# Taking GpSimd's reads of SBUF out of the pooling stage of a two-layer encoder step

## The chip, the cores and the metric

One launch on one core of a Trainium2 chip. The metric is the device time of that launch in microseconds (us), as the median of several runs. The five engines of the core are TensorE (PE in the profile; PEld is its weight load), VectorE (DVE), ScalarE (ACT), GpSimd (POOL) and SyncE (SP, which here only issues DMAs).

## The reference, cut to what matters

Two equal layers work on 576 columns: 512 frames of a new stream ("prompt") and 64 further frames of a running stream ("sample", with 1024 cached frames). All numbers are float32.

```
h = rms_norm(x, norm_g);  proj = h @ w_in            # 1024 inputs, 5416 columns of weights
u_p, z_p, q, k, v, qi, ki, wi, z_a, g_p, g_a = split(proj)
pooled   = for 4 groups of 128 channels: mean over the last 2, 4, 8, 16 frames of u_p, minus u_p
br_pool  = ((pooled @ w_pool_mix) * pool_scale * silu(z_p)) @ w_pool_out
score    = sum_heads wi * relu(rope(qi) @ rope(ki).T * 32**-0.5) * 8**-0.5
sel      = the best 128 (prompt) or 256 (sample) keys of each row of score
o        = softmax over sel of rope(q) @ rope(k).T * 64**-0.5, times v
x        = x + (sigmoid(g_p) * br_pool + sigmoid(g_a) * ((o * silu(z_a)) @ w_attn_out)) @ w_o
```

The new keys, values, indexer keys and the last 15 rows of u_p are outputs too. After layer 2 a last rms_norm gives y.

## The kernel before, in words

Channels lie on the 128 partitions and the 576 columns along the free dimension, as two halves of 288. Weights come in pieces of 128 x 1024 float32 (512 KB), 58 in each layer. TensorE takes float32 operands rounded to its own format, so each operand is split into a rounded high part and a low part (value minus high part), and each product is made of three matmuls: high by high, high by low, low by high. One piece is 48 matmuls of 288 columns. The high part of a piece is made by a ScalarE copy; the low part by a second, negated ScalarE copy, onto which a DMA of the POOL queue adds the raw piece (`split_to`). The first piece alone is done by halves with subtractions on VectorE and GpSimd (`split_first`). Raw pieces have a ring of three buffers (`raws`), split pieces a ring of three (`whl`).

Everything is issued through a planner (`Plan`, lines 66 to 250). It keeps an estimated free time for each engine from a cost formula for each operation, and it emits waiting jobs (`pump`) between the matmuls of a product where it believes that their inputs are ready. So the estimates set the order of the instructions on every engine, and an engine then runs its list strictly in that order. The formulas hold no term for one engine slowing another. `psum_free`, `need` and `room` are its conditions; four PSUM banks ("sm") serve small products and two double banks ("mm") the weight products.

The stages of a layer, in the order of the pieces:

- **Entry.** x is rounded (`h`), its low part made, and squared (`sq`); the squares are summed in `acc` for the norm. In layer 1 this runs while x arrives (`first`); `FIRST_H` names the k for which VectorE rounds instead of ScalarE, and `FIRST_POOL` those whose square GpSimd adds. The same eight steps multiply the key weights `kiw` and the first query piece. `norm_a` reduces `acc` by matmuls with ones and takes the root, `norm_b` spreads the result over all partitions as `Rt`.
- **Pooling stage.** Pieces u0 to u3 and z0 to z3 (`u_job`, `z_job`). VectorE scales the product (`ux`), builds window sums and `pl`; ScalarE rounds `pl` into `ph`; the low part follows. z is turned into a gate `sg` (sigmoid on ScalarE, then a product). Six matmuls per group mix (`sm<-quart 128x288` in the trace), and the result `av` is split into `ah` and `al`. Between these stand the index scores: 24 products for the prompt (`sm<-quart,big`, 256, 384 and 512 columns wide), each passed by ScalarE as relu into a `prob` buffer and added up by VectorE (`SCALAR_TENSOR_TENSOR quart<-prob,wcol,quart`).
- **Selection.** VectorE alone: 16 rounds of MAX8 and MATCH_REPLACE8 for the prompt, then 12 sample score products of 364 or 360 columns, then 32 rounds for the sample. The result of the sample's selection is needed only by the sample attention at the end.
- **Gates, attention, outputs.** gp, po, then k, q, v pieces with the prompt's attention between them, then za, ga with the sample's attention, then the two output products. GpSimd has the rotary products of k and other products there.

In the pooling stage of before, GpSimd does the small copies into `ux` and `pst`, the low parts of `ph`, of the mixing weights `wmx` and of `al`, and the gate product. At the end of layer 1, `prepare_ki` loads the next layer's raw key weights into one of the three `raw` buffers.

All operations go through one recording helper, so every instruction has line L263; the tile names tell them apart.

Of the kernel before, what the change touches and what calls it, by code (L numbers as in the profile page):

```python
# [10 lines left out]
F32 = mybir.dt.float32  # L11
F32R = mybir.dt.float32r
AF = mybir.ActivationFunctionType
OP = mybir.AluOpType
# [3 lines left out]
TP = 512  # L18
TS = 64
T = TP + TS  # L20
# [26 lines left out]
UNITS = 3  # L47
FIRST_H = (1, 3, 5, 7)
FIRST_POOL = (1, 2, 3)
LAG = (1, 2)  # L50
# [218 lines left out]
def encoder_step(ctx: ExitStack, tc: tile.TileContext, a: dict):  # L269
# [86 lines left out]

    def split_first():

        x = raw_of.pop(0)
        w = rot.tile([P, 2, 1024], F32R, name="whl", tag="whl", bufs=3)  # L360
        for c, eng in ((slice(0, 512), dve), (slice(512, 1024), pool)):
            act.copy(w[:, 0, c], x[:, c])
            eng.tensor_tensor(w[:, 1, c], x[:, c], w[:, 0, c].bitcast(F32), op=OP.subtract)
        plan.let(x)
        split_of[0] = w
        state["split"] = 1

# [178 lines left out]
    def prepare_ki(l):  # L546
        rk = raws()
        rki = rk[:, :320].rearrange("p (k c) -> p k c", k=8)
        dma.dma_start(rk[:, :320], a["w_ki"][l])

        def ki_split():
            act.copy(kiw[:, :, 0:40], rki)
            (pool if l else dve).tensor_tensor(kiw[:, :, 64:104], rki, kiw[:, :, 0:40].bitcast(F32), op=OP.subtract)
            plan.let(rk)

        return ki_split

    def layer(l, x, arrive):
# [24 lines left out]
        for k in range(8 + lag[1]):  # L583
# [14 lines left out]
            if k >= lag[1]:  # L598
                step(ps_q0, w, xh, xl, k - lag[1], 8, low=(True,))
                plan.pump()  # L600
            if l == 0 and k in (4, 6):
                split_to(k // 2)
        kt = tmp()
# [11 lines left out]
        for k in range(8):  # L615
            step(ps_q1, w, xh, xl, k, 8)
            plan.pump()
            if k == NORM_A:
                x.norm_a()
                sh0 = swapped(ps_q0[:, :, :HT])  # L620
            if k == NORM_B:
                x.norm_b()
# [62 lines left out]
        def ki_stack():  # L685
# [23 lines left out]
            act.copy(wmx[:, 0:512], wm[:, :512])  # L709
            yield lambda: need("pool", wmx, room=1.0)  # L710
            pool.tensor_tensor(wmx[:, 512:1024], wm[:, :512], wmx[:, 0:512].bitcast(F32), op=OP.subtract)
            let(wm)
# [134 lines left out]
        def u_job(g):  # L847
            ps = block(xh, xl)
            ux = tmp(608)
            pool.memset(ux[:, 0:PST], 0.0)  # L850
            pool.tensor_copy(ux[:, PST + TP:2 * PST + TP], spool[:, l, g])
            dve.tensor_tensor(ux[:, PST:PST + HT], ps[:, 0, :HT], Rt[:, :HT], op=OP.mult)
# [5 lines left out]
            def go():  # L858
                yield lambda: need("pool", ux)
                pool.tensor_copy(pst[:, g, 0], ux[:, TP:TP + PST])  # L860
                pool.tensor_copy(pst[:, g, 1], ux[:, W - PST:W])
                s, lo = ux, 0
# [15 lines left out]
                act.copy(ph[:, TP:T], pl[:, TP + PST:n])  # L878
                yield lambda: need("pool", ph[:, :T])
                pool.tensor_tensor(ph[:, T:T + TP], pl[:, :TP], ph[:, :TP].bitcast(F32), op=OP.subtract)  # L880
                pool.tensor_tensor(ph[:, T + TP:], pl[:, TP + PST:n], ph[:, TP:T].bitcast(F32), op=OP.subtract)
                pooled[g] = ph
# [8 lines left out]
        def z_job(g):  # L891
# [4 lines left out]
            def go():  # L896
                sg = tmp()
                yield lambda: need("act", zt)
                act.activation(sg, zt, AF.Sigmoid)
                yield lambda: need("pool", sg)  # L900
                pool.tensor_tensor(sg, sg, zt, op=OP.mult)
                yield lambda: g in pooled and "wm" in done and psum_free(2) and need("pe", pooled[g], wmx) and need("dve", sg, room=ROOM)
# [21 lines left out]
                act.copy(ah[g // 2][:, c], av)  # L924
                yield lambda: need("pool", ah[g // 2][:, c])
                pool.tensor_tensor(al[g // 2][:, c], av, ah[g // 2][:, c].bitcast(F32), op=OP.subtract)

# [658 lines left out]
```

## Time and profile before

| | |
|---|---|
| median of 3 runs | 941.17 us (940.51 to 943.63) |
| profiled execution | 936.12 us; span of its instructions 934.4 us |
| TensorE busy / mean granted clock | 901.1 us (96%) / 0.986 |
| VectorE, ScalarE, GpSimd busy | 656.4, 605.0, 303.5 us |

The profile is one execution. Its span runs from the first to the last instruction. A row of a timeline gives the start, the length, the engine, the operation, the tiles (out<-in), the shapes and how many instructions were merged; in brackets stands how long the engine idled before and what ended that wait. A matmul's recorded length includes time in the pipeline, so a busy TensorE may still be late. The granted clock is a share of TensorE's full 2.4 GHz; the other level is 1.2 GHz, 0.5 of it.

### The profile page before, as it was taken

How to read it: one execution, taken by the hardware profiler on the slowest of the kernel's cores; microseconds unless marked ns; L12 is line 12 of the kernel's file. 1: busy time of each engine (PE TensorE's matmuls, PEld its weight loads, DVE VectorE, ACT ScalarE, POOL GpSimd, SP SyncE). 2: the span in 40 equal slices, each digit the busy share in tenths (PEclk: the TensorE clock that was granted, in tenths of full speed). 3: DMA queues.
4: the chain of work that ended last, by engine and by line, in shares of the span. 5: the costliest groups of instructions: out<-in, count | busy, mean ns of one | idle time of the engine just before them, and what ended most of it. 6: DMA issues, size and time to landing. Idle time of an engine off the chain costs nothing.

```text
span 934.4 us, 17465 instructions
## 1 busy us (share of the span) xinstructions
PE 901.1 (96%) x6613; PEld 887.2 (95%) x6613; DVE 656.4 (70%) x1488; ACT 605.0 (65%) x1060; POOL 303.5 (32%) x310
## 2 busy tenths in 40 slices
PE   7999999999999999999999999999999999999996
PEld 6998999999999999999999999999989899999995
DVE  7787899798984467362249779969898745754414
ACT  6455555668889966565545655474898997656642
POOL 5144553434341310112124536435443132001121
PEclk7999999999999999999999999999999999999998
DMA  9655577775555685688976556877665467758862
GB/s 284 170 122 122 142 187 204 176 178 149 155 151 139 143 218 156 185 217 214 251 209 164 133 127 170 215 179 194 165 145 122 119 152 198 204 144 223 231 157 102
DMA packets 54644, 161.49 MB, mean 173 GB/s; under 512 B 6752, under 2 KB 9056, under 8 KB 54560
## 3 DMA queue, kind: packets, MB, share of 16 engines
q0 software_dynamic: 16560, 60.30, 34.4%
q1 hardware_dynamic: 38000, 100.08, 32.0%
q8 instruction: 52, 0.85, 0.4%
q14 instruction: 32, 0.26, 0.1%
HBM read 85.37 MB, written 14.69 MB: 107 GB/s over the span
## 4 chain that ended last, share of the span: by engine, by line
PE 60%; DVE 25%; ACT 7%; issue 4%; DMA 3%; POOL 1%; SPq 0%; DVEq 0%; ACTq 0%; POOLq 0%
PE mm L263 49%; DVE quart L263 13%; PE sm L263 11%; DVE tmp L263 10%; DMA raw<-in_w_dram 2%; ACT whl L263 2%; ACT prob L263 1%; ACT quart L263 1%; DMA whl<-raw 1%; ACT tmp L263 1%; POOL tmp L263 1%; DVE qzl L263 1%; DVE prob L263 0%; ACT big L263 0%; ACT qz L263 0%
## 5 line engine op out<-in xcount | busy, mean ns | idle before, releaser
L263 PE MATMUL mm<-quart,whl 128*128 128x288 f32 (+1 forms) x5568 | 786.5, 297 | 3.4 <-DVE tmp L263 2.6
L263 PEld LDWEIGHTS mm<-quart,whl 128*128 128x128 f32 x5568 | 759.7, 189 | 6.3 <-PE mm L263 2.0
L263 POOL DMA_DIRECT2D whl<-raw x115 | 100.9, 877 | 520.1 <-ACT whl L263 398.0
L263 ACT CAST whl<-raw 128x1024 fp32r<-128x1024 f32 (+1 forms) x117 | 121.6, 1040 | 62.7 <-PE mm L263 37.5
L263 ACT ACTIVATE whl<-raw 128x1024 fp32r<-128x1024 f32 x115 | 121.5, 1056 | 0.0
L263 DVE SCALAR_TENSOR_TENSOR quart<-prob,wcol,quart 128x256 f32<-128x256 f32 (+4 forms) x60 | 56.9, 961 | 26.5 <-ACT prob L263 23.5
L263 ACT ACTIVATE prob<-prob,stat 128x512 f32<-128x512 f32 (+3 forms) x128 | 68.4, 555 | 8.4 <-DVE stat L263 7.6
L263 ACT CAST quart<-tmp 64x512 fp32r<-64x512 f32 (+4 forms) x44 | 24.1, 565 | 57.4 <-DVE tmp L263 45.8
L263 ACT COPY tmp<-mm 128x576 f32<-128x576 f32 x40 | 25.4, 635 | 48.2 <-PE mm L263 47.9
L263 POOL TENSOR_TENSOR quart<-tmp,quart 64x512 fp32r<-64x512 f32 (+3 forms) x40 | 50.7, 1315 | 15.6 <-ACT quart L263 14.9
L263 DVE TENSOR_TENSOR big<-sm,big 128x512 fp32r<-128x512 f32 (+1 forms) x64 | 29.6, 485 | 32.6 <-ACT big L263 32.1
L263 POOL TENSOR_TENSOR tmp<-tmp 128x576 f32<-128x576 f32 x32 | 50.0, 1562 | 4.0 <-ACT tmp L263 3.1
L263 DVE MATCH_REPLACE8 quart<-stat,quart 128x256 f32<-128x256 f32 (+2 forms) x96 | 51.3, 547 | 0.0
L263 DVE MAX8 stat<-quart 128x8 f32<-128x256 f32 (+2 forms) x96 | 47.4, 550 | 0.0
L263 DVE MAX8 quart<-quart 128x8 f32<-128x544 f32 x64 | 46.3, 723 | 1.4
L263 DVE MATCH_REPLACE8 quart<-quart 128x544 f32<-128x544 f32 x64 | 45.3, 709 | 0.0
L263 ACT ACTIVATE prob<-sm 128x256 f32<-128x256 f32 (+4 forms) x72 | 31.9, 482 | 16.9 <-PE sm L263 16.8
L263 DVE TENSOR_TENSOR tmp<-tmp 128x576 f32<-128x576 f32 (+7 forms) x54 | 40.9, 763 | 1.9
L263 DVE TENSOR_TENSOR quart<-quart 128x576 fp32r<-128x576 f32 (+5 forms) x28 | 25.1, 895 | 20.0 <-ACT quart L263 18.8
L263 ACT COPY prob<-sm 64x512 f32<-64x512 f32 (+1 forms) x24 | 12.3, 513 | 39.4 <-PE sm L263 39.1
L263 ACT CAST big<-sm 128x512 fp32r<-128x512 f32 (+2 forms) x72 | 28.4, 430 | 9.7 <-PE sm L263 9.2
L263 POOL TENSOR_TENSOR tmp<-tmp,Rt 128x576 f32<-128x576 f32 x16 | 23.5, 1467 | 32.1 <-ACT tmp L263 32.1
(159 smaller groups left out, 1049.7 us busy)
## 6 DMA issues: line engine op xcount, KB each, us to landing
raw<-in_w_dram SPq DMA_DIRECT2D x116, 512.0 KB, 4.7
whl<-raw POOLq DMA_DIRECT2D x115, 512.0 KB, 4.8
mp<-tmp SPq DMA_DIRECT2D x16, 288.0 KB, 3.2
tmp<-mp SPq DMA_DIRECT2D x16, 288.0 KB, 5.0
prob<-in_c_k_dram SPq DMA_DIRECT2D x16, 256.0 KB, 4.8
prob<-in_c_v_dram SPq DMA_DIRECT2D x16, 256.0 KB, 3.0
out_o_v_dram<-quart SPq DMA_DIRECT2D x8, 320.0 KB, 4.0
quart<-in_x_dram SPq DMA_DIRECT2D x8, 288.0 KB, 6.2
```

Of the source, the lines that this page charges most:

```text
L263: return f(*args, **kw)
```

## The change

1. In the pooling stage, eight kinds of operation go from GpSimd to others: the low parts of `wmx`, `ph`, `al` and the gate product go to VectorE, the copies into `ux` and `pst` go to ScalarE. GpSimd keeps a MEMSET of 15 columns for each group and the issue of the weight DMAs.
2. At the entry of layer 1, ScalarE rounds all eight parts of x (before, VectorE did four), VectorE adds all squares (before, GpSimd did three). The second weight piece is split by halves like the first, without a DMA. `norm_a` moves from behind k = 0 of the second query product to behind k = 2, and `norm_b` from k = 3 to k = 4.
3. The raw key weights lie in a `prob` buffer instead of a `raw` buffer, in both layers.

```
-FIRST_H = (1, 3, 5, 7)
-FIRST_POOL = (1, 2, 3)
+FIRST_H = ()
+FIRST_POOL = ()
...
-    def split_first():
-
-        x = raw_of.pop(0)
+    def split_first(i=0):
+
+        load_to(i + 1)
+        x = raw_of.pop(i)
...
-        split_of[0] = w
-        state["split"] = 1
+        split_of[i] = w
+        state["split"] = i + 1
...
     def prepare_ki(l):
-        rk = raws()
+        rk = prob()
...
-            plan.let(rk)
...
-            if l == 0 and k in (4, 6):
-                split_to(k // 2)
+            if l == 0 and k == 4:
+                split_first(1)
+            if l == 0 and k == 6:
+                split_to(3)
...
+            if k == (NORM_A if l else 2):
+                x.norm_a()
             if k == NORM_A:
-                x.norm_a()
                 sh0 = swapped(ps_q0[:, :, :HT])
-            if k == NORM_B:
+            if k == (NORM_B if l else 4):
                 x.norm_b()
...
-            yield lambda: need("pool", wmx, room=1.0)
-            pool.tensor_tensor(wmx[:, 512:1024], wm[:, :512], wmx[:, 0:512].bitcast(F32), op=OP.subtract)
+            yield lambda: need("dve", wmx, room=1.0)
+            dve.tensor_tensor(wmx[:, 512:1024], wm[:, :512], wmx[:, 0:512].bitcast(F32), op=OP.subtract)
...
-            pool.tensor_copy(ux[:, PST + TP:2 * PST + TP], spool[:, l, g])
+            act.copy(ux[:, PST + TP:2 * PST + TP], spool[:, l, g])
...
-                yield lambda: need("pool", ux)
-                pool.tensor_copy(pst[:, g, 0], ux[:, TP:TP + PST])
-                pool.tensor_copy(pst[:, g, 1], ux[:, W - PST:W])
+                yield lambda: need("act", ux)
+                act.copy(pst[:, g, 0], ux[:, TP:TP + PST])
+                act.copy(pst[:, g, 1], ux[:, W - PST:W])
...
-                yield lambda: need("pool", ph[:, :T])
-                pool.tensor_tensor(ph[:, T:T + TP], pl[:, :TP], ph[:, :TP].bitcast(F32), op=OP.subtract)
-                pool.tensor_tensor(ph[:, T + TP:], pl[:, TP + PST:n], ph[:, TP:T].bitcast(F32), op=OP.subtract)
+                yield lambda: need("dve", ph[:, :T])
+                dve.tensor_tensor(ph[:, T:T + TP], pl[:, :TP], ph[:, :TP].bitcast(F32), op=OP.subtract)
+                dve.tensor_tensor(ph[:, T + TP:], pl[:, TP + PST:n], ph[:, TP:T].bitcast(F32), op=OP.subtract)
...
-                yield lambda: need("pool", sg)
-                pool.tensor_tensor(sg, sg, zt, op=OP.mult)
+                yield lambda: need("dve", sg)
+                dve.tensor_tensor(sg, sg, zt, op=OP.mult)
...
-                yield lambda: need("pool", ah[g // 2][:, c])
-                pool.tensor_tensor(al[g // 2][:, c], av, ah[g // 2][:, c].bitcast(F32), op=OP.subtract)
+                yield lambda: need("dve", ah[g // 2][:, c])
+                dve.tensor_tensor(al[g // 2][:, c], av, ah[g // 2][:, c].bitcast(F32), op=OP.subtract)
```

Since the planner sees other costs, it also sets another order from the pooling stage on. Three places follow; names are as in the trace.

VectorE at the entry of layer 1, before: rounding (TENSOR_SCALAR) and low parts (SCALAR_TENSOR_TENSOR) alternate, and four squares are added at the end.

```order
L263 TENSOR_SCALAR quart<-quart,gains 128x576
L263 SCALAR_TENSOR_TENSOR quart<-quart,gains 128x576 x2
L263 TENSOR_SCALAR quart<-quart,gains 128x576
L263 SCALAR_TENSOR_TENSOR quart<-quart,gains 128x576
L263 TENSOR_TENSOR acc<-tmp,acc 128x576 x4
L263 TENSOR_TENSOR tmp<-sm,tmp 40x288 x2
```

The same place now, with half of the second weight piece (`whl`) in front of the last low part:

```order
L263 TENSOR_TENSOR whl<-raw,whl 128x512
L263 SCALAR_TENSOR_TENSOR quart<-quart,gains 128x576 x5
L263 TENSOR_TENSOR whl<-raw,whl 128x512
L263 SCALAR_TENSOR_TENSOR quart<-quart,gains 128x576
L263 TENSOR_TENSOR acc<-tmp,acc 128x576 x7
L263 TENSOR_TENSOR tmp<-sm,tmp 40x288 x2
```

No rounding is left in VectorE's list, and three more additions of squares stand behind the last low part.

VectorE in the pooling stage, at pieces z0 and z1, before (`tmp<-mm,Rt` takes z out of its PSUM bank, `tmp<-sm,pscale,tmp` is the mixed result times the gate):

```order
L263 SCALAR_TENSOR_TENSOR quart<-prob,wcol,quart 128x384 x2
L263 TENSOR_TENSOR tmp<-mm,Rt 128x576
L263 SCALAR_TENSOR_TENSOR quart<-prob,wcol,quart 128x384 x3
L263 SCALAR_TENSOR_TENSOR tmp<-sm,pscale,tmp 128x288 x2
L263 SCALAR_TENSOR_TENSOR quart<-prob,wcol,quart 128x384
```

The same place now; `quart<-tmp,quart 128x576` is the low part `al`, `tmp<-tmp 128x576` the gate product:

```order
L263 TENSOR_TENSOR quart<-tmp,quart 128x576
L263 TENSOR_TENSOR tmp<-mm,Rt 128x576
L263 SCALAR_TENSOR_TENSOR quart<-prob,wcol,quart 128x384
L263 TENSOR_TENSOR tmp<-tmp 128x576
L263 SCALAR_TENSOR_TENSOR tmp<-sm,pscale,tmp 128x288 x2
L263 SCALAR_TENSOR_TENSOR quart<-prob,wcol,quart 128x384 x2
```

The two operations that GpSimd had stand in VectorE's list now, and the score additions between them are spread out.

TensorE at the end of the prompt's scores and at the first sample scores (`sm<-quart 128x364`), before:

```order
L263 MATMUL sm<-quart,big 128x512
L263 MATMUL mm<-quart,whl 128x288 x6
L263 MATMUL sm<-quart 128x288 x6
L263 MATMUL mm<-quart,whl 128x288 x54
L263 MATMUL sm<-quart 128x288 x6
L263 MATMUL mm<-quart,whl 128x288 x348
L263 MATMUL sm<-quart 128x364
```

The same place now:

```order
L263 MATMUL sm<-quart,big 128x512
L263 MATMUL mm<-quart,whl 128x288 x6
L263 MATMUL sm<-quart,big 128x512
L263 MATMUL mm<-quart,whl 128x288 x396
L263 MATMUL sm<-quart 128x364
```

All four mixing products now stand ahead of the last scores. Counted from the start of the layer, the first sample score has 78 more matmuls of 288 columns ahead of it than before.

## Rows read from the trace of the kernel before

**Rows 1.** The page's parts 1 and 2: TensorE's busy time, its granted clock in 40 slices.

```profile
PE 901.1 (96%) x6613; PEld 887.2 (95%) x6613; DVE 656.4 (70%) x1488; ACT 605.0 (65%) x1060; POOL 303.5 (32%) x310
PEclk7999999999999999999999999999999999999998
```

**Rows 2.** Stretches (us): busy time of each engine, granted clock, DMA share, GB/s.

```profile
50.00:100.00 50.00, 47.55 (x337) 46.72 (x335) 39.02 (x62) 28.23 (x50) 22.85 (x31) 0.97 0.51 129
200.00:250.00 50.00, 48.28 (x356) 46.83 (x355) 45.98 (x119) 43.39 (x94) 20.64 (x20) 1.00 0.59 153
250.00:300.00 50.00, 47.78 (x355) 46.73 (x354) 36.58 (x104) 45.61 (x104) 13.67 (x14) 1.00 0.55 135
```

**Rows 3.** TensorE's timeline in the pooling stage, the last row from layer 2.

```profile
81.54 0.67 PE L263 MATMUL sm<-quart 128*128 128x288 f32 x3 [1.93 <-ACT prob L263]
...
82.22 4.88 PE L263 MATMUL mm<-quart,whl 128*128 128x288 f32 x24
...
100.09 1.16 PE L263 MATMUL sm<-quart 128*128 128x288 f32 x6 [0.61 <-ACT prob L263]
...
108.44 1.03 PE L263 MATMUL mm<-quart,whl 128*128 128x288 f32 x6 [0.80 <-DVE tmp L263]
...
535.63 0.66 PE L263 MATMUL sm<-quart 128*128 128x288 f32 x3 [1.98 <-ACT prob L263]
```

**Rows 4.** The chain that ended last: start, us, what.

```profile
110.26 46.40 PE mm L263 x348
```

**Rows 5.** Timelines of VectorE and GpSimd in the pooling stage.

```profile
76.46 0.62 DVE L263 SCALAR_TENSOR_TENSOR quart<-prob,wcol,quart 128x384 f32<-128x384 f32 x1
...
89.69 3.58 DVE L263 SCALAR_TENSOR_TENSOR quart<-prob,wcol,quart 128x384 f32<-128x384 f32 x1 [2.46 <-ACT prob L263]
...
100.07 6.17 DVE L263 SCALAR_TENSOR_TENSOR quart<-prob,wcol,quart 128x512 f32<-128x512 f32 x4 [2.38 <-ACT prob L263]
...
89.73 1.74 POOL L263 TENSOR_TENSOR quart<-tmp,quart 128x576 fp32r<-128x576 f32 x1
91.13 1.72 POOL L263 TENSOR_TENSOR tmp<-tmp 128x576 f32<-128x576 f32 x1
```

**Rows 6.** Groups by shape, 25 to 115 us: count, busy us, mean ns, idle before.

```profile
L263 DVE SCALAR_TENSOR_TENSOR quart<-prob,wcol,quart 128x384 f32<-128x384 f32 x7 | 8.9, 1269 | 5.9 <-ACT prob L263 5.6
...
L263 DVE TENSOR_TENSOR tmp<-tmp 128x576 f32<-128x576 f32 x4 | 3.0, 752 | 0.1
...
L263 ACT CAST quart<-tmp 128x64 fp32r<-128x64 f32 x4 | 1.0, 241 | 0.0
```

**Rows 7.** ScalarE's timeline ahead of the long wait of TensorE.

```profile
79.13 1.28 ACT L263 ACT_TABLE_LOAD   x1
```

**Rows 8.** Timelines of four engines at the entry of layer 1.

```profile
6.15 0.81 DVE L263 SCALAR_TENSOR_TENSOR quart<-quart,gains 128x576 fp32r<-128x576 f32 x1
...
13.44 2.58 DVE L263 SCALAR_TENSOR_TENSOR quart<-quart,gains 128x576 fp32r<-128x576 f32 x2
...
11.16 3.52 POOL L263 TENSOR_TENSOR acc<-tmp,acc 128x576 f32<-128x576 f32 x2
...
12.92 0.76 ACT L263 ACTIVATE quart<-quart,gains 128x576 fp32r<-128x576 f32 x1
...
15.35 0.85 PE L263 MATMUL sm<-quart,kiw 128*128 128x288 f32 x2 [0.71 <-DVE quart L263]
```

**Rows 9.** Stretches of 5 us at the entry, as in Rows 2.

```profile
10.00:15.00 5.00, 3.59 (x17) 3.01 (x15) 4.93 (x4) 5.00 (x9) 4.60 (x3) 0.59 1.04 411
15.00:20.00 5.00, 4.65 (x19) 4.66 (x20) 4.92 (x8) 3.61 (x5) 1.88 (x2) 0.50 0.98 277
```

**Rows 10.** The end of layer 1: SyncE's issue of the key weights, TensorE's wait.

```profile
438.93 0.66 SPq L263 DMA_DIRECT2D raw<-in_w_ki_dram  x1
...
462.73 6.39 PE L263 MATMUL mm<-quart,whl 128*128 128x288 f32 x46 [0.80 <-DMA whl<-raw]
```

**Rows 11.** TensorE's longest wait in the attention of layer 1.

```profile
281.47 0.33 PE L263 MATMUL sm<-quart,qz 128*128 128x128 f32 x1 [2.11 <-DVE big L263]
```

## The prediction

> **What bounds the kernel now.** I read the page's busy shares first, then stretches of the span, then TensorE's timeline with its waits, then VectorE's and GpSimd's timelines beside each wait. TensorE is busy for 901.1 of 934.4 us [rows 1], so a change can win only what TensorE now loses: waits, and stretches at the 1.2 GHz clock. The clock's row shows such stretches at the ends alone, but a tenth is coarse: the stretch from 50 to 100 us has 0.97 [rows 2]. That is the pooling stage of layer 1, where the change sits. Three waits there are 1.93, 0.61 and 0.80 us long, two for a PSUM bank that ScalarE has yet to empty (`prob`), one for VectorE (`tmp`) [rows 3]. Behind the first wait 24 matmuls of a weight product take 4.88 us [rows 3]; at full clock 348 take 46.40 us, 0.133 each [rows 4], so 24 would take 3.20. The lower clock costs 1.68 us there. The stage loses 1.93 + 0.61 + 0.80 + 1.68 = 5.0 us. Layer 2 repeats it, with a first wait of 1.98 us [rows 3]: some 10 us for both.
>
> Why are these waits there? A score addition of 384 columns takes 0.62 us alone, and 3.58 us at 89.69 [rows 5]. In that time GpSimd runs two operations that read SBUF, one from 89.73 for 1.74 us, the next from 91.13 for 1.72, ending at 92.85. VectorE's addition ends at 93.27, 0.42 behind. It stood still until GpSimd was done with both. From 100.07 four additions of 512 columns take 6.17 us beside another such pair [rows 5]. Seven additions of 384 columns average 1269 ns [rows 6], so they lose 7 x (1.269 - 0.62) = 4.5 us in this one group. The order was planned without this term: VectorE falls behind it, ScalarE waits for VectorE's sums, and then a table load of 1.28 us [rows 7] and TensorE's products come upon late banks.
>
> **The pooling stage.** Per layer, VectorE receives four gate products and four low parts `al` of 576 columns, 8 x 0.752 = 6.0 us [rows 6], and four low parts `ph` and one of `wmx` of about the same size, an estimate of 5 x 0.75 = 3.8 by the same row: 9.8 us. It loses the stalls: 4.5 us in the 384-column group, and at 100.07 alone about 6.17 - 4 x 0.75 = 3.2 more; the window sums and other additions have further ones that I did not sum. So VectorE's load stays about where it was, 39.0 of 50 us [rows 2] and at most 9.8 - 7.7 = 2.1 us more, with the difference that the planner knew of this load when it set the order. ScalarE receives 12 copies of 15 columns; the nearest row is a cast of 64 columns, 241 ns [rows 6], so at most 2.9 us, into an engine that is busy for 28.2 of 50 us [rows 2]. GpSimd was off the path except through VectorE; its weight DMAs now have no subtraction in front of them, and they were not waited for here.
>
> What comes instead of the 10 us? If nothing is late, all of it is won; if VectorE has no room for the 9.8 us, nothing is. In the new order the score additions are spread between gate products and low parts, where before they stood in runs. I keep 2 us of small waits (two of the 0.5 us kind in each layer; the shortest of the three above is 0.61) and take -8.0, between -10.0 and 0.
>
> The Trainium skill, page "Perfetto Trace Analysis", section "Optimizing Scalar/DVE Operations", says that where VectorE is saturated, moving work to ScalarE or even GpSimd may make sense, but that between VectorE and GpSimd it might not help because they share a read port of SBUF. The first half speaks against this change, which moves work to the busier engine; the second half is for it, and the addition of 3.58 us above is on the side of the second. By the first half the -8.0 would be 0 or worse; that is the second rival below.
>
> **The entry of layer 1.** VectorE's low parts take 0.81 us alone; two take 2.58 beside GpSimd's additions of squares (3.52 us from 11.16), and TensorE waits 0.71 us for them at 15.35 [rows 8]. With neither GpSimd's additions nor VectorE's roundings, the low part of k = 3 is ready near 12.7 instead of 15.3 (it starts once the one of k = 2 has ended, at about 11.8, and takes 0.81). ScalarE then sets the pace: a rounding is 0.76 us [rows 8] and the square of the same size behind it somewhat less, 1.4 us for both as an estimate; and it has the second weight piece ahead of k = 7. TensorE runs at the lower clock from 10 to 20 us (0.59 and 0.50) [rows 9], where the ten matmuls of one k take 2.7 us, so TensorE and not ScalarE is late for most of it. I get the last step of the entry about 2 us earlier. Against it stands the later norm: `norm_b` has six more matmuls of 0.133 us ahead of it, and the chain of VectorE operations behind it is the one that TensorE waits for next; so 0.8 us are given back. Taken: -1.2. Bounds: if the clock came back at once, the 10 us at 0.59 and 0.50 give up to -4.5; if it stays low over two steps more, 2 x 1.33 = +2.7. VectorE's three more additions of squares, 3 x 0.75 = 2.3 us, lie beside TensorE's last steps; if that cover is gone, they are in the upper bound too.
>
> **Key weights in another buffer.** At the end of layer 1 they take one turn of the three raw buffers at 438.93, and TensorE waits 0.80 us for a weight piece at 462.73 [rows 10]. With a turn free, the pieces behind it start earlier. Taken: -0.8; bounds 0 (the DMAs are late anyway) and -1.0. In layer 1 the first load is alone and nothing changes.
>
> **The attention.** The sample's scores move behind 78 more matmuls of 288 columns, 78 x 0.133 = 10.4 us of TensorE work. So about 10 us of the sample's selection, which VectorE did while it had little else, come to the stretch from 200 to 300 us. There VectorE idles 4.0 us in the first half and 13.4 in the second [rows 2], so it fits, but the prompt's attention shares the engine, and TensorE's longest wait there, 2.11 us, is for VectorE [rows 11]. The order of attention is another one, too, so that wait may vanish or others come. Per layer between -1.5 and +4; taken +0.75, so +1.5 for both.
>
> **Sum.** -8.0 - 1.2 - 0.8 + 1.5 = -8.5 us. The profiled execution took 936.1 us, so it would take 927.6; it lies 5.0 us under the median of 941.2, and I keep that distance: 932.7 us. About 0.3% (2.8 us) is what a measurement of this kernel can tell from no change, so faster means under 938.4.
>
> **Rivals.**
> 1. *The waits come back in another place.* VectorE's load is unchanged by my count, and ScalarE's table load and weight casts are all still there. Then the pooling stage wins only the time at the lower clock that went with the long wait, 2 x 1.7 = 3.4, and the rest as above: -3.4 - 0.5 = -3.9 us, 937.3; without the entry's gain 938.5. For it: the banks are still four. Against it: ScalarE was late because VectorE was. Chance 0.13.
> 2. *VectorE becomes the bound* (slower). The place is from the first `ph` to the middle of the attention. If the 9.8 us find no room, the pooling stage wins nothing and the selection ends late; what of the 10.4 us does not fit into the 4.0 idle us of the first half of the attention, 6.4 us, TensorE waits for, in each layer: +12.8 - 1.2 - 0.8 = +10.8 us, 952. It decides from the point where VectorE idles under 1 us in 50 between 100 and 250 us, with TensorE's waits there naming VectorE. For it: 46.0 of 50 us busy. Against it: the stalls that go are nearly as long as the work that comes. Chance 0.07.
> 3. *The entry wins much more*, because TensorE is fed without a gap and the clock returns early: -4.5 instead of -1.2, sum -11.8, 929.4. Chance 0.12.
> That GpSimd's remaining MEMSETs and DMA issues stall VectorE as before, so that the change does not do what it says, I count within rival 1.
>
> **How the numbers follow.** The forecast's case has 0.68, rivals 0.13, 0.07 and 0.12. The likeliest case's own range: lowest -10.0 - 1.2 - 1.0 - 3.0 = -15.2, 926; highest with half the pooling gain, no entry gain and +4 for attention, -4 - 0.8 + 4 = -0.8, 940. The range 926 to 940 leaves out rival 2, and of the forecast's case its tails, together under 0.2. Faster: 0.95 of the forecast's case, rival 3 and half of rival 1, 0.65 + 0.12 + 0.06 = 0.83. Same: 0.03 + 0.06 + 0.01 = 0.10. Slower: 0.07.
>
> **What would show it.** Pooling: score additions of 384 columns near 0.62 us on average, no wait of TensorE over 1 us between 40 and 110 us, and granted clock 1.00 from 25 us on. Entry: no wait of TensorE at k = 3, and the granted clock back at 1.00 before 20 us. Key weights: no wait for `whl` near 460 us. Attention: VectorE over 46 us busy in 200 to 250, TensorE's waits there within 2 us of before. It would be wrong if waits for VectorE appear in the pooling stage where those for ScalarE were, or if attention loses more than 4 us in a layer.

## The result, and the profile after

The changed kernel takes 925.73 us (median of 4 runs, 924.12 to 926.23) beside 940.84 for the kernel before: 0.9837 of its time, with a 95% interval of 0.9804 to 0.9871. That is 15.1 us less, where 8.5 were forecast; the range ended at 926.0, 0.3 us above the measured median. The profiled execution took 925.37 us (span 923.4), and so lies at the median, not 5 us below it as that of before did.

The page of the kernel after, its parts 1 and 2, beside [rows 1]: GpSimd falls from 303.5 to 246.4 us, TensorE's clock row differs in its first digit alone.

```profile
PE 897.9 (97%) x6613; PEld 883.5 (96%) x6613; DVE 654.0 (71%) x1522; ACT 609.4 (66%) x1088; POOL 246.4 (27%) x249
...
PEclk8999999999999999999999999999999999999998
```

Stretches of the kernel after, columns as in [rows 2]; the last two answer to [rows 9].

```profile
50.00:100.00 50.00, 50.00 (x374) 49.82 (x373) 39.12 (x75) 30.48 (x57) 9.10 (x11) 1.00 0.64 157
200.00:250.00 50.00, 48.58 (x361) 47.55 (x360) 44.74 (x119) 42.84 (x96) 20.04 (x20) 1.00 0.61 152
250.00:300.00 50.00, 49.94 (x369) 48.59 (x368) 43.19 (x118) 44.84 (x100) 15.84 (x16) 1.00 0.58 146
10.00:15.00 5.00, 4.48 (x16) 3.91 (x17) 3.65 (x5) 5.00 (x9) 1.28 (x1) 0.50 1.03 411
15.00:20.00 5.00, 5.00 (x35) 5.00 (x34) 3.81 (x5) 3.40 (x6) 1.29 (x1) 0.85 0.66 235
```

In the pooling stage TensorE issues 374 matmuls in 50 us instead of 337, at full clock, and VectorE is as busy as it was (39.12 us against 39.02), though it now does the work that GpSimd gave up.

TensorE's timeline of the kernel after, columns as in [rows 3]: its waits at the entry, ahead of the pooling stage, in it, and the longest in the attention.

```profile
10.01 1.33 PE L263 MATMUL mm<-quart,whl 128*128 128x288 f32 x4 [1.20 <-ACT whl L263]
...
39.50 3.43 PE L263 MATMUL mm<-quart,whl 128*128 128x288 f32 x24 [1.35 <-DVE tmp L263]
...
101.22 0.50 PE L263 MATMUL sm<-quart,big 128*128 128x512 f32 x1 [0.71 <-DVE tmp L263]
...
323.68 0.33 PE L263 MATMUL sm<-ident,prob 128*128 128x128 f32 x1 [1.48 <-ACT prob L263]
```

Of the three waits of [rows 3] in layer 1 none is left; one of 0.71 us stands in their place. The wait of 1.35 us at 39.50, ahead of the stage, comes with the new entry; in the kernel before it is 0.45 us. So 0.9 us are given back there, near the 0.8 that the prediction took for the later norm. Groups of the kernel after by shape, 25 to 115 us, as in [rows 6]:

```profile
L263 DVE SCALAR_TENSOR_TENSOR quart<-prob,wcol,quart 128x512 f32<-128x512 f32 x7 | 9.3, 1331 | 3.0 <-ACT prob L263 2.7
L263 DVE TENSOR_TENSOR tmp<-tmp 128x576 f32<-128x576 f32 x8 | 6.0, 752 | 0.1
L263 DVE SCALAR_TENSOR_TENSOR quart<-prob,wcol,quart 128x384 f32<-128x384 f32 x7 | 4.3, 616 | 3.2 <-ACT prob L263 3.2
...
L263 ACT COPY pst<-tmp 128x15 f32<-128x15 f32 x8 | 1.3, 205 | 0.1
```

The score additions of 384 columns have gone from a mean of 1269 ns to 616, which is their time alone. Those of 512 columns have not: their mean is 1331 ns. One of them shows why. Timelines of VectorE and GpSimd after:

```profile
96.31 3.56 DVE L263 SCALAR_TENSOR_TENSOR quart<-prob,wcol,quart 128x512 f32<-128x512 f32 x1 [1.80 <-ACT prob L263]
...
101.51 0.74 DVE L263 SCALAR_TENSOR_TENSOR quart<-prob,wcol,quart 128x512 f32<-128x512 f32 x1
```

```profile
96.18 1.75 POOL L263 TENSOR_TENSOR Ct<-tmp,Rt 128x576 f32<-128x576 f32 x1
97.58 1.73 POOL L263 TENSOR_TENSOR St<-tmp,Rt 128x576 f32<-128x576 f32 x1
```

Two products that the change left on GpSimd hold up one addition for 2.8 us, until both are done. It is the pattern of [rows 5]; in the stage as a whole it is left at a few places where before it came again and again.

To place the gain I compare the starts of six products that every version has, with the same work of TensorE between them: A, the second set of 448-column products of layer 1; B, its first attention product; C, the first key weight product of layer 2; D and E, the same as A and B in layer 2; F, the last two transposes. (Only A has 0.8 us more work ahead in the changed kernel, and A to B has 0.8 less.) The columns "before, again" and "after, again" are profiles of the unchanged two kernels from the experiments.

| stretch, us | before | before, again | key weights alone | after | after, again |
|---|---|---|---|---|---|
| start to A (entry of layer 1) | 47.36 | 44.74 | 45.21 | 45.99 | 44.43 |
| A to B (pooling, selection) | 154.29 | 154.28 | 154.30 | 149.55 | 149.60 |
| B to C (attention to the last product) | 267.31 | 273.85 | 267.30 | 266.34 | 266.47 |
| C to D (entry of layer 2) | 32.44 | 32.42 | 32.40 | 32.39 | 32.39 |
| D to E (pooling, selection) | 154.40 | 154.37 | 154.35 | 150.47 | 150.51 |
| E to F (attention to the end) | 271.54 | 272.95 | 272.80 | 271.92 | 271.98 |

Three things stand out. The pooling stages give 3.9 to 4.7 us each, in every pair. The pooling stage of the kernel before takes the same 154.3 us whether the granted clock from 50 to 100 us is 0.97 [rows 2] or 1.00, as in the profile "before, again". And the kernel before can lose another 6.5 us between B and C, which the profile that I had been shown did not contain.

### The profile page after: what moved, and what is told of

Same layout as the page of the kernel before. It is cut to its first block, busy times and chain, and to the rows that moved or that the text cites. A ratio compares the mean times of both kernels' runs of the same rounds, so it can differ in the third digit from the quotient of the medians.

```text
span 923.4 us, 17457 instructions
## 1 busy us (share of the span) xinstructions
PE 897.9 (97%) x6613; PEld 883.5 (96%) x6613; DVE 654.0 (71%) x1522; ACT 609.4 (66%) x1088; POOL 246.4 (27%) x249
## 4 chain that ended last, share of the span: by engine, by line
PE 72%; DVE 12%; ACT 10%; issue 3%; POOL 1%; DMA 1%; SPq 0%; DVEq 0%; POOLq 0%; ACTq 0%
PE mm L263 61%; PE sm L263 12%; DVE quart L263 6%; DVE tmp L263 4%; ACT whl L263 3%; ACT prob L263 3%; ACT quart L263 2%; POOL tmp L263 1%; ACT qz L263 1%; DMA raw<-in_w_dram 1%; ACT tmp L263 1%; DVE big L263 1%; DVE prob L263 0%; SPq L263 0%; DVE tau L263 0%
## 5 line engine op out<-in xcount | busy, mean ns | idle before, releaser
L263 ACT ACTIVATE prob<-prob,stat 128x384 f32<-128x384 f32 (+3 forms) x128 | 68.0, 554 | 4.1 <-DVE stat L263 3.7
L263 DVE SCALAR_TENSOR_TENSOR quart<-prob,wcol,quart 128x256 f32<-128x256 f32 (+4 forms) x60 | 46.3, 776 | 29.9 <-ACT prob L263 29.0
L263 ACT ACTIVATE prob<-sm 128x256 f32<-128x256 f32 (+4 forms) x72 | 33.8, 482 | 46.9 <-PE sm L263 46.9
L263 DVE TENSOR_TENSOR quart<-quart 128x576 fp32r<-128x576 f32 (+6 forms) x30 | 30.3, 1009 | 18.6 <-ACT quart L263 18.3
L263 POOL TENSOR_TENSOR tmp<-tmp 128x576 f32<-128x576 f32 x24 | 36.2, 1508 | 2.0 <-ACT tmp L263 0.8
L263 PE MATMUL sm<-quart,big 128*128 128x128 f32 (+3 forms) x176 | 32.2, 291 | 1.4 <-DVE tmp L263 1.4
```

The costliest lines, as they stand in the source:

```text
L263: return f(*args, **kw)
```

## The experiments

All ran in rounds with the kernel before; ratios are to that kernel, with 95% intervals.

**The kernel before again.** No edit.

> The kernel before, unchanged, to see what lies between its profiled execution (936.1 us) and its median (941.2). Theory A (the distance is TensorE's clock, which falls after long waits in some executions and not in others): the slower executions show a lower mean granted clock than 0.986; a stretch of d us at 1.2 GHz costs d/2, so 5 us more of time go with a clock lower by about 5/935 = 0.005, that is 0.980 to 0.982. Theory B (the distance is waits, for DMA for instance): the granted clock stays at 0.985 to 0.987 in all executions while the span moves by 5 us.

Measured: 941.07 us, 0.9999 (0.9979 to 1.0018), 12 executions from 937.2 to 944.7, mean clocks from 0.990 (the 937.2) to 0.983 (the 944.7). So the clock does move with the time, as theory A had it. The cause is another one than A's. TensorE's timeline and one stretch of this profile:

```profile
457.67 15.37 PE L263 MATMUL mm<-quart,whl 128*128 128x288 f32 x94 [3.19 <-DMA whl<-raw]
```

```profile
380.00:470.00 90.00, 86.67 (x632) 86.16 (x631) 32.95 (x49) 47.41 (x62) 14.29 (x16) 0.96 0.83 216
```

The wait for a weight piece that took 0.80 us in [rows 10] takes 3.19 here, and 94 matmuls behind it take 15.37 us, where 94 x 0.133 = 12.5 would do: 2.9 us more at the lower clock, 6.1 together. The pooling stage's clock was 1.00 from 50 to 100 us in this execution; its waits were those of [rows 3] and one more of 0.57 us, and the stage was as long. The three profiles of kernels with the key weights in a raw buffer that were taken here have waits of 3.19, 2.78 and 3.58 us at this place. The 0.80 of the profile I read was the exception.

**The three parts, each alone.**

```
pooling alone:      the changed kernel with the old FIRST_H, FIRST_POOL, split_first,
                    norm_a and norm_b, and rk = raws()
entry alone:        the kernel before with the new FIRST_H, FIRST_POOL, split_first,
                    norm_a and norm_b
key weights alone:  the kernel before with
-        rk = raws()
+        rk = prob()
-            plan.let(rk)
```

> Part 1 of the change alone (pooling stage); entry and key weights as before. In the two profiles the pooling stages gained 4.9 us each and the attention lost 1.05 and 1.1. Theory A (the median's further 4 us are clock lost behind the long waits of the pooling stage): median 7.7 + 4 = about 11.7 us under before, 929, with a spread of the runs under 3 us. Theory C (the further 4 us sit at the entry): 7.7 us under before, 933, and the spread stays at 5 us or more.

> Part 2 alone (entry of layer 1). In the two profiles the entry gained about 2.2 us. Theory A: median about 2 us under before, 939, waits of the pooling stage as before (a first one near 1.9 us for ScalarE's prob). Theory C (the distance between profile and median sits at the entry): about 6 us under, 935. My prediction had -1.2: 940.

> Part 3 alone (raw key weights in a prob buffer). In the two profiles the stage with w_o and the key weights of layer 2 gained 1.25 us; predicted -0.8. Both theories: 0 to -1.3 us against before, within what can be measured. A rival: with the raw buffer free the pieces of layer 1 also come earlier, or the prob buffer held by the key weights delays the scores; then more than 3 us in either direction.

Measured:

| | us (runs) | ratio (95%) | difference |
|---|---|---|---|
| pooling alone | 931.84 (928.9 to 935.1) | 0.9909 (0.9881 to 0.9938) | -8.6 (-11.2 to -5.8) |
| entry alone | 940.01 (938.5 to 942.2) | 0.9990 (0.9974 to 1.0007) | -0.9 (-2.4 to +0.7) |
| key weights alone | 935.97 (934.7 to 937.3) | 0.9953 (0.9935 to 0.9971) | -4.4 (-6.1 to -2.7) |

The parts add up to -13.9, about the -15.1 of the whole. Theories A and C both fail: the pooling part neither reaches 929 nor loses its spread (6 us), the entry is not 6 us faster, and the last of the three, which I thought too small to measure, gives 4.4. It also takes the spread away: 9 executions within 2.6 us, where the kernel before has 7.4. The rival in its expectation had the size, but not the way: what it speeds up is neither layer 1's first pieces nor the scores.

SyncE's timeline of the kernel before again; its waits for `whl<-raw` from 430 to 470 us (total, number, longest); two rows of GpSimd; then SyncE's timeline of the key weights alone:

```profile
437.92 0.66 SPq L263 DMA_DIRECT2D raw<-in_w_ki_dram  x1
439.49 0.33 SPq L263 DMA_DIRECT2D raw<-in_w_dram  x1
...
447.82 0.33 SPq L263 DMA_DIRECT2D raw<-in_w_dram  x1
...
449.19 0.44 SPq L263 DMA_DIRECT2D raw<-in_w_dram  x1
```

```profile
SPq L263 <- DMA whl<-raw: 5.0, 2, 4.2
```

```profile
442.00 0.88 POOL L263 TENSOR_TENSOR kiw<-raw,kiw 128x320 fp32r<-128x320 f32 x1
449.47 0.88 POOL L263 DMA_DIRECT2D whl<-raw  x1 [6.59 <-ACT whl L263]
```

```profile
438.02 0.71 SPq L263 DMA_DIRECT2D prob<-in_w_ki_dram  x1
438.83 0.46 SPq L263 DMA_DIRECT2D raw<-in_w_dram  x1
...
443.76 0.67 SPq L263 DMA_DIRECT2D raw<-in_w_dram  x1
...
451.52 0.76 SPq L263 DMA_DIRECT2D raw<-in_w_dram  x1
```

The weight piece behind the next one is issued 8.3 us after it instead of 4.9, and the piece behind that one 1.4 us later instead of 7.8. Not the key weights' own buffer is late: GpSimd is done with it at 442.88. By the buffers' addresses in the two programs, the late load takes the buffer of the piece just ahead of the key weights, and with the key weights elsewhere it takes that of one piece earlier. SyncE waits until the DMA that adds that piece onto its low part (`whl<-raw`) has landed.

TensorE's wait is not for one of these two loads but for the piece ahead of them, loaded at 439.49. Its `whl<-raw` DMA starts at 449.47, beside the two loads, and takes 8.2 us to land, where it takes 5.5 with the key weights alone. It is 8.7 and 8.8 us in pooling alone and entry alone, where the two loads are 1.4 us apart, too, and 4.6 to 6.3 in all other profiles but one below. In the profile of [rows 10] the two loads were 2.9 us apart and this DMA took 6.3; why they lay further apart there is open.

**GpSimd's reads put back, and its time without reads.** At the three places per group at which GpSimd had work (until its table products), and nowhere else:

```
reads:   + nc.gpsimd.tensor_tensor(x.acc, x.acc, x.acc, op=OP.subtract)
writes:  + nc.gpsimd.memset(x.acc, 0.0)
         + nc.gpsimd.memset(x.acc[:, :288], 0.0)
```

> The changed kernel, with one more GpSimd operation at each of three places per pooling group at which GpSimd had work before (13 per layer): acc - acc into acc, 576 columns, whose result nothing uses. The orders of TensorE, VectorE and ScalarE stay those of the changed kernel, so only GpSimd's reading is put back. Theory (VectorE stands still while GpSimd reads SBUF): score additions of 384 columns go from a mean of 616 ns to over 900, VectorE's 13 x 1.7 = 22 us of GpSimd time beside 75% busy VectorE cost it some 8 us per layer, waits of TensorE for VectorE or ScalarE return in both pooling stages: +4 to +10 us on 925.7, so 930 to 936. Rival (the gain came from the new order alone): 925 to 927.

> The changed kernel, with two GpSimd MEMSETs of acc (576 and 288 columns) at the same 13 places per layer: GpSimd is kept busy and its weight DMAs are kept waiting for a similar time, but it reads no SBUF. Theory (reading counts): score additions of 384 columns stay near 616 ns, time 925 to 927. Rival (a busy GpSimd counts, by its late weight DMAs or by writing): as slow as the kernel with the reads, 930 to 936.

Measured: with reads 940.80 us, 1.0005 (0.9987 to 1.0023); with writes 924.64, 0.9830 (0.9806 to 0.9854). The reads cost as much as the whole change gains; the writes cost nothing. (That the first comes out at the very time of the kernel before is chance: it keeps the gain of the key weights, and its pooling stage is slower than the old one, 157.19 us from A to B against 154.29, since VectorE has the work now and GpSimd reads all the same. Ten operations stand in each layer, not the 13 of the expectation, since the table products come ahead of the last three places.) Groups by shape, 25 to 115 us, and the stretch from 50 to 100 us, first with the reads:

```profile
L263 DVE TENSOR_TENSOR tmp<-tmp 128x576 f32<-128x576 f32 x8 | 8.9, 1106 | 0.1
L263 DVE SCALAR_TENSOR_TENSOR quart<-prob,wcol,quart 128x384 f32<-128x384 f32 x7 | 6.4, 910 | 2.9 <-ACT prob L263 2.9
L884 POOL TENSOR_TENSOR acc<-acc 128x576 f32<-128x576 f32 x4 | 5.9, 1468 | 0.1
L934 POOL TENSOR_TENSOR acc<-acc 128x576 f32<-128x576 f32 x3 | 4.2, 1415 | 0.2
L907 POOL TENSOR_TENSOR acc<-acc 128x576 f32<-128x576 f32 x3 | 4.1, 1377 | 0.1
```

```profile
50.00:100.00 50.00, 45.43 (x321) 44.73 (x320) 41.52 (x69) 25.55 (x51) 18.25 (x18) 0.95 0.56 140
```

Then with the writes:

```profile
L263 DVE TENSOR_TENSOR tmp<-tmp 128x576 f32<-128x576 f32 x8 | 6.0, 752 | 0.1
L263 DVE SCALAR_TENSOR_TENSOR quart<-prob,wcol,quart 128x384 f32<-128x384 f32 x7 | 4.3, 616 | 3.2 <-ACT prob L263 3.2
```

```profile
50.00:100.00 50.00, 49.74 (x370) 49.33 (x368) 39.06 (x74) 29.70 (x56) 18.27 (x31) 1.00 0.62 151
```

GpSimd is busy for 18.25 and 18.27 us of the 50 in the two, and the orders of TensorE, VectorE and ScalarE are those of the changed kernel. The added work itself is not quite equal, 14.2 us of products against 10.9 us of MEMSETs in the stage; both write `acc`, and the products alone read. TensorE's waits with the reads are these:

```profile
77.14 0.44 PE L263 MATMUL sm<-quart,big 128*128 128x384 f32 x1 [2.09 <-ACT prob L263]
...
97.36 0.50 PE L263 MATMUL sm<-quart,big 128*128 128x512 f32 x1 [2.48 <-DVE tmp L263]
```

From A to B the version with reads takes 157.19 us against 149.60, and from D to E 158.07 against 150.51: 7.6 us in each layer, for ten operations that take 14.2 us on GpSimd. VectorE loses 7 x (0.910 - 0.616) = 2.1 us in the additions of 384 columns and 8 x (1.106 - 0.752) = 2.8 in the other group; with the window sums and the low parts of `ph` it is 8.9 in the stage. The rest of the way is that of the kernel before: ScalarE's `prob` and TensorE's bank are late. In layer 1 TensorE waits for 2.09 and 2.48 us where the changed kernel waits for 0.71, and the clock is 0.89 from 75 to 105 us, which is 3.3 us. That makes 2.09 + 2.48 - 0.71 + 3.3 = 7.2 of the 7.6. In layer 2 the clock is 1.00 from 490 to 545 us, and more waits stand in its place: 2.00, 0.79, 0.41, 2.51 and 1.50, together 7.2, which is 6.5 more than in the changed kernel. The loss is the same, so it is set by how late VectorE is, and the lower clock is not a further loss on top of it.

No run has the old order without the reads. How much of the 8.6 us of the pooling part the new order alone would give is therefore not shown.

The Trainium skill, page "SBUF — State Buffer", section "Who interferes with whom", says that a VectorE instruction with two inputs in SBUF contends with a GpSimd instruction that reads SBUF, and not with one that only writes it. The two runs agree, 940.80 against 924.64 us.

**A turn of the raw buffers, without and with holding it.** The key weights stay in `prob`; a load of 12 KB takes a raw buffer beside them.

```
     rk = prob()
+    if l:                                  # both; in the second behind the key weights' load
+        rt = raws(); dma.dma_start(rt[:, :24], a["gains"])
+        plan.let(rt)                       # first version
...
     (pool if l else dve).tensor_tensor(kiw[:, :, 64:104], rki, ...)
+    if l:                                  # second version, in place of the let above
+        pool.memset(rt[:, :24], 0.0); plan.let(rt)
```

> The changed kernel, whose key weights stay in the prob buffer, with one turn of the three raw buffers taken in layer 1 at the place where the key weights stood: a load of 24 columns (12 KB) goes into it and is not used. Theory (the turn itself counts: the second weight piece behind it must wait for a piece that leaves its buffer one step later): TensorE waits 2 to 3.5 us for whl near 450 us and the clock falls behind that, +3 to +5 us on 925.7, so 929 to 931. Rival (the 160 KB of the key weights or the time they hold the buffer count): 925 to 927, no wait.

> As the run with one turn of the raw buffers given back, but the buffer is now held as long as the key weights held it: a load of 24 columns (12 KB) goes into it right behind the key weights' load, and it is let go behind the subtraction on GpSimd that splits the key weights (a MEMSET of 24 columns stands there). Theory (what costs is that one of three buffers is held for about 5 us, so that the next weight piece but one is loaded 4 us later): the load of raw behind it is issued 8 us after the one ahead of it instead of 4.8, TensorE waits 2 to 3.5 us for whl, time 928.5 to 931. Rival (the 160 KB in the raw buffer's place in the queue, or something else in the kernel before): 925 to 927 and no such wait.

Measured: the turn alone 925.87 us, 0.9843 (0.9819 to 0.9868), no loss that the runs can tell. Held, 930.12 us (926.8 to 931.7), 0.9872 (0.9845 to 0.9900), where the changed kernel in the same rounds has 924.46 and 0.9822 (0.9796 to 0.9848): 4.7 us by the ratios, 5.7 by the medians. SyncE's timeline with the turn alone, then with the buffer held, and TensorE's with it held:

```profile
434.24 0.33 SPq L263 DMA_DIRECT2D raw<-in_w_dram  x1
438.40 1.01 SPq L263 DMA_DIRECT2D raw<-in_w_dram  x1
...
447.69 0.65 SPq L263 DMA_DIRECT2D raw<-in_w_dram  x1
```

```profile
433.91 0.33 SPq L263 DMA_DIRECT2D raw<-in_w_dram  x1
442.50 0.33 SPq L263 DMA_DIRECT2D raw<-in_w_dram  x1
...
443.87 0.44 SPq L263 DMA_DIRECT2D raw<-in_w_dram  x1
```

```profile
451.62 14.18 PE L263 MATMUL mm<-quart,whl 128*128 128x288 f32 x94 [2.47 <-DMA whl<-raw]
```

Here are the 8 us between two loads again (8.6), the next load 1.4 us behind, and the wait, without the 160 KB of the key weights in the raw buffer. The piece that TensorE waits for needs 8.6 us for its `whl<-raw` DMA again; with the turn alone it needs 4.6.

Why did the first version cost nothing? It let the buffer go at once, and by the addresses in its program the second piece behind it takes that very buffer. So it did not bring back the turn of the kernel before, and it says nothing against the theory in its expectation. In the held version, as in the kernel before, the extra load is one more turn of the ring: the second piece behind it takes the buffer of the piece just ahead, and must wait one piece longer. The held buffer itself is free again at 437.73, 4.8 us before that load. So by these traces the price is the turn and not the time that the buffer is held: SyncE, whose list is strictly in order, waits for a piece that is split later, and two loads then run beside the DMA that TensorE needs next. The spread of the runs comes back with it, too (5 us, against 2.0 for the changed kernel).

**TensorE kept busy at the entry.**

```
+FILL = {0: 3, 1: 9, 2: 4}
...      behind the low key weight products of each half
+                if l == 0:
+                    for _ in range(FILL.get(k, 0)):
+                        nc.tensor.matmul(warm[:, :P], lhsT=mask0, rhs=mask0, start=True, stop=True)
```

> The changed kernel, with 3, 9 and 4 matmuls of 128 columns of a constant into a bank that nobody reads behind the key weight products of k = 0, 1 and 2 of layer 1, in place of TensorE's waits of 0.3 and 1.2 us there. Theory (the clock falls at 9.7 us because TensorE idles, and the stretch to 17 us at 1.2 GHz costs about 3 us): clock 1.00 through the entry, the last key weight product 1 to 1.5 us earlier (x and ScalarE's roundings come at 1.24 us a step), time 923 to 925. Rival (the clock falls whatever TensorE does there, or the filler delays the product that waits): 925.5 to 927.5.

Measured: 924.21 us, 0.9830 (0.9802 to 0.9857). The two stretches that answer to [rows 9] have the full clock, and the last key weight product starts at 18.45 instead of 20.76:

```profile
10.00:15.00 5.00, 5.00 (x42) 5.00 (x41) 3.73 (x5) 5.00 (x9) 0.39 (x1) 1.00 1.04 411
15.00:20.00 5.00, 5.00 (x40) 5.00 (x39) 4.16 (x6) 2.93 (x6) 1.30 (x1) 1.00 0.83 293
```

The span is 1.2 us shorter than that of the changed kernel's first profile; but the second profile of that kernel had its last key weight product at 19.12 and the same span as this. And three profiles with this entry and no filler (the entry alone, the reads put back, the tables on VectorE below) have a clock of 1.00 in both stretches, too. So neither the full clock nor the 1.2 us can be put down to the filler.

**The last two reads of the pooling stage taken away.** The products for `Ct` and `St` go to VectorE (`pool.tensor_tensor(t, raw, Rt, ...)` becomes `dve.tensor_tensor`); the last run has the filler as well.

> The changed kernel once more, so that the two that follow can be set beside it on one chip: 925 to 927.

> The changed kernel, with the two products that make the tables Ct and St (576 columns each, once per layer) on VectorE instead of GpSimd. In the trace of the changed kernel they run on GpSimd from 96.18 to 99.31 us, a score addition beside them takes 3.56 us instead of 0.74, and TensorE then waits 0.71 us for VectorE. Theory (the last contention of the pooling stage): that wait goes, VectorE gains 2.8 - 1.5 = 1.3 us per layer, time 0.7 to 2 us under the changed kernel, 924 to 925. Rival (it comes back in the attention): same as the changed kernel within 0.7 us.

> The same with the filler matmuls at the entry of layer 1 as well. If both gains are real and add up (filler: the last key weight product 2.3 us earlier, 1.2 us in the span; tables: 1 to 2), 922 to 924; if the filler's gain is lost to the waits behind the entry, as the run with the tables alone.

Measured: the changed kernel again 924.46 us, 0.9822 (0.9796 to 0.9848); tables 923.63, 0.9808 (0.9782 to 0.9834); tables and filler 923.13, 0.9804 (0.9778 to 0.9830). With the tables on VectorE, VectorE's timeline has

```profile
94.15 0.75 DVE L263 TENSOR_TENSOR Ct<-tmp,Rt 128x576 f32<-128x576 f32 x1
94.81 0.75 DVE L263 TENSOR_TENSOR St<-tmp,Rt 128x576 f32<-128x576 f32 x1
...
97.27 0.74 DVE L263 SCALAR_TENSOR_TENSOR quart<-prob,wcol,quart 128x512 f32<-128x512 f32 x1
```

and TensorE no wait between 80 and 125 us. The wait of 0.71 us is gone, as expected; the time is 0.8 us less (1.3 with the filler), at the lower end of what I expected and inside the intervals. The stage shows it more clearly: A to B and D to E are 0.9 to 1.0 us shorter in both profiles with the tables on VectorE (148.6 and 149.5 us), and E to F is 0.3 to 0.4 longer. Each of the five runs with the tables alone also lies under each of the five of the changed kernel beside them (922.34 to 923.94 against 924.10 to 926.11). That the filler adds anything to this is not shown.

## Why the prediction was wrong

Its direction and its main mechanism were right. The step that failed is the price of the key weights, and with it the distance kept to the median; the attention had the wrong sign, by less. Of the 6.6 us between -8.5 and -15.1, 3.6 are the key weights', 2.1 those of part 1 (pooling stage and attention, taken -8.0 + 1.5 = -6.5, measured -8.6 with an interval from -11.2 to -5.8); the entry gave 0.3 less than taken, and 1.2 us are not placed, since the parts add up to -13.9.

- **Where TensorE loses time, and the pooling stage: right but for one term.** The waits and the low clock of the pooling stage were the largest term. Taken -8.0; A to B and D to E give -3.9 (0.8 us less work taken off) and -3.9. The signs were as listed: score additions of 384 columns at 616 ns, no wait over 1 us between 40 and 110 us, VectorE as busy as before. The runs with reads and writes show that GpSimd's reading costs this stage. One term of the working does not hold: the 1.68 us at the lower clock are not a loss of their own. With the clock at 1.00 the stage of the kernel before is as long (154.28 against 154.29 us), and other waits fill the place. So the 3.4 us that rival 1 keeps stand for nothing by themselves, and that -8.0 comes so near to -7.8 is in part luck.
- **The entry: right by the part alone** (taken -1.2, measured -0.9 with an interval to both sides of nothing). The clock was back before 20 us, as forecast: 0.85 from 15 to 20 us, and 1.00 from 18 to 20. The fall is not fixed to the kernel: in the profile of the kernel before again the same two stretches have 0.71 and 1.00, where [rows 9] have 0.59 and 0.50.
- **The attention: wrong in sign, and small.** Taken +1.5 for the 10.4 us of selection that move into it. B to C and E to F came out at -0.97 (with the wait of 0.80 us of [rows 10] in it) and +0.38 between the first two profiles, at -0.8 and -0.8 from the key weights alone to the changed kernel again. VectorE took the selection into its idle time, not from 200 to 250 us, where over 46 us were forecast and 44.74 came, but from 250 to 300 us (43.19 us busy, before 36.58), and the wait of 2.11 us [rows 11] went with the new order; one of 1.48 us came. So VectorE did not become the bound, and nothing was lost.
- **The key weights: the step that failed.** "Taken: -0.8; bounds 0 (the DMAs are late anyway) and -1.0": measured -4.4 (-6.1 to -2.7). I had the mechanism, "With a turn free, the pieces behind it start earlier", but took the wait of one profiled execution, 0.80 us [rows 10], as its price, and left out both that the wait differs between executions and the clock that falls behind a longer one. In the other profiles with this turn the wait is 2.78 to 3.58 us, and it comes with 94 matmuls at a lower clock (2.9 us more in the one shown). The bound of -1.0 had no reason but that one row. What the profiles show in place of the 0.80 us is a late load with the next one 1.4 us behind it, and a `whl<-raw` DMA that takes 8.2 to 8.8 us beside the two. [Rows 10] held the sign: a wait for a DMA, whose length depends on what else the DMAs do at that moment.
- **"It lies 5.0 us under the median of 941.2, and I keep that distance": the same error once more.** I took the distance between the profile and the median as something that both kernels have. It was for the most part a loss of the kernel before, and this loss is in the part that the change takes away: with the key weights alone the profiled execution took 935.14 us and the median is 935.97. The distance should have been a question: which wait of this profile may be longer in the other runs? [Rows 9] and [rows 10] named the clock of the entry and a DMA; the DMA it was.

Of the rivals none came in. The first (waits come back elsewhere) was -3.9; the third (the entry wins much more) came near the number, 929.4, by another way than the one that happened.

## What to carry to other kernels

Where VectorE adds up two operands from SBUF, look at GpSimd's reads beside one long instance of it, and give GpSimd work that only writes or issues, even when VectorE looks busy: here the time it gained back paid for the work. A ring of buffers that feeds a stage with busy DMAs should hold nothing but the pieces it is made for: each tensor that takes a turn in it makes loads behind it wait for a piece that is used later, unless its buffer can be taken again at once. And a profile that is faster than the median of its kernel's runs can hide a loss: find the wait that can be longer before you carry the difference over.

## What the runs showed of the hardware

- An addition of 512 columns waited for two GpSimd products one after the other (3.56 us from 96.31, products from 96.18 to 99.31), not only for the one that ran when it began.
- GpSimd's MEMSETs of 576 and 288 columns did not lengthen VectorE's additions at all (616 ns with and without), over 10.9 us of MEMSETs in the stage.
- The clock at the entry differs between executions of one program: 0.59 and 0.50 in the two stretches from 10 to 20 us of one profile of the kernel before, 0.71 and 1.00 in the next; the stretch from the start to A took 47.36 and 44.74 us. A difference of 2.6 us there is within what one program shows from one profile to the next.
- In the pooling stage a lower clock behind a wait cost no time of its own: 154.29 us at 0.97 and 154.28 at 1.00 in two profiles of one program.
- A `whl<-raw` DMA of 512 KB landed after 4.6 to 6.3 us where the next two weight loads were 6.9 to 9.3 us apart, and after 8.2 to 8.8 us in the four profiles where they were 1.4 us apart.
